# A two-layer attention and pooling trunk on one core: operand offsets in attention, a norm spread one chunk later, squares and running sums reordered, last scalings split up

## The chip, the cores and the metric

The kernel runs on 1 core of one Trainium2 chip. The metric is the device time of one execution in microseconds (us); the median of several runs counts. The engines of the core work side by side, each through its own queue in order: TensorE (PE, with its weight loads as PEld), VectorE (DVE), ScalarE (ACT), GpSimd (POOL) and SyncE (SP, which only issues transfers here). They wait for each other through semaphores.

## The reference

The input `x` is one sequence of 512 positions by 1024 channels in float32. Two layers follow each other, and each sub-layer adds its result to `x`:

```
x = x + dilated_attention_mixer(rmsnorm(x, attn_norm), w_qkv, w_attn_out)   # 24 heads in 3 groups
x = x + swiglu_ffn(rmsnorm(x, ffn_norm[0]), w_gate_up[0], w_down[0])        # d_ff = 2816
x = x + pooling_mixer(rmsnorm(x, pool_norm), w_pool_in, w_pool_group, pool_scale)
x = x + swiglu_ffn(rmsnorm(x, ffn_norm[1]), w_gate_up[1], w_down[1])
return rmsnorm(x, final_norm)
```

`rmsnorm` divides each position by the root of the mean of its squares over the channels. The pooling mixer projects to 4 groups of 256 channels, takes in each group the mean over the last 2, 4, 8 or 16 positions minus the position itself, and applies a 256 x 256 map per group. All arithmetic is float32.

## The kernel before

**Layout.** The state is held transposed: eight tiles `X[0..7]`, each 128 channels by 512 positions. A product is 128 output channels by 512 positions in one PSUM tile (`ps`, 8 buffers) and runs over the eight chunks of the contraction.

**Three matmuls for one.** A float32 operand is split into a rounded part and the rest (`split`, line 92: ACT writes the rounded part at L93, DVE subtracts it at L94). Every chunk then takes three matmuls: high weight by high operand, high by low, low by high. In `Product.add` these are L314, L315 and L317, with 512 columns each. Large products are done with fewer multiplications on quarter blocks (Strassen's scheme): `mult` issues L446, L447 and L448 with 256 columns each, and the sums of blocks are made on DVE. `values12` does the same for the values of attention (L617 to L619), with the weights as the moving operand and the activations as the stationary one.

**Weights.** They stream from memory into rings `raw` and `rawhalf` (SP's queue, and for sums of blocks POOL's) and are split into rings `w` (5 buffers) and `half`. A ring buffer is 64 float32 elements (`LINE`) longer than the weights, and `shift` says at which element of a partition's row the weights begin. `pairs(..., shift=LINE // 4)` puts the weights of attention's block products at element 16.

**Operands.** Split operands lie in slots of 2 x 512 elements in two rooms, `near` and `far`; a slot taken with `apart=True` begins `APART` = 28 elements later. The feed-forward layers use it, attention doesn't: its operands (`near`, `h`, and `tx` in the tiles of `X`) begin at element 0. So the moving operand begins 16 elements (64 bytes) below its weights in attention's block products, 28 elements (112 bytes) above them in the feed-forward layers and in `values12`, and at the same offset in plain products. All other steps of these buffers are multiples of 256 bytes.

**Order.** Instructions are written in one program; a scheduler lays them out per engine by its own priorities, so their order on an engine is not always that of the code. Stages follow each other:

1. Start (0 to 33 us): for each chunk k, `X[k]` and the weights of four products are loaded, split, and multiplied; `square(0, k)` squares the chunk on ACT (L367) and adds it up on DVE (L369).
2. Attention (to 480 us): heads two by two, with block products (`seven`), and between their steps scores, softmax and outputs of the head before, as small matmuls.
3. Feed-forward 0 (to 809 us), pooling (to 868 us), feed-forward 1 (to 1170 us). The norm between two stages is `finish`: it ends two products that were begun ahead, adds up the squares of a column over the partitions by matmuls with `ones` (`rstd`, L396), takes the power -1/2 on POOL (L402), runs three chunks of a further product (`begin(1, layer, range(3))`), and spreads the factors over the partitions by matmuls with the identity (`spread`, L409). Consumers scale the products by that `row` when they leave PSUM.
4. Pooling: `pool(g)` for g = 3, 2, 1, 0 takes two products each (L1217), makes the sum over the last 2^(g+1) positions by g + 1 shifted additions on DVE (L1225), finishes the mean (L1229 to L1233) and splits it; `mix(g)` multiplies by the group's map, adds to `X` (L1242), and makes the operands (L378 on ACT, L379 on DVE) and squares of the next norm. The order is pool 3, pool 2, mix 3, pool 1, mix 2, pool 0, mix 1, mix 0.
5. End (from 1170 us): the last five down products are done by halves of the positions (`end`, `add`: L1280 adds to `X`, L1282 squares on ACT, L1318 adds up). `emit(0, r)` scales the eight tiles of the first half (L1291) and writes them out (L1292). The second half is scaled by the norm weight (`scale_last`, L1305 or L1303), turned by PE (`turn_last`, L1313), multiplied by the factor (L1349, L1351) and written out (L1352).

The sums of the pooling windows, and the first norm's order, are these lines:

```
for k in range(KC):
    ...
    nc.scalar.activation(hi[:, s], raw[:, s], AF.Copy)
    scaled(0, k, *U[k], on_dve=k == 0)
    nc.vector.tensor_tensor(lo[:, s], raw[:, s], hi[:, s].bitcast(F32), op=OP.subtract)
    for i, f in enumerate(lead):
        f.w = (hi, lo)
        f.add([k], pos=k % 2 * NF + i - k)
    square(0, k)
```

Of the kernel before, what the change touches and what calls it, by code (L numbers as in the profile page):

```python
# [8 lines left out]
F32 = mybir.dt.float32  # L9
# [6 lines left out]
P = 128  # L16
# [31 lines left out]
LINE = 64  # L48
APART = 28
# [15 lines left out]
def trunk(ctx: ExitStack, tc: tile.TileContext, xT, xN, norms, w_first, w_qk, w_qkp, w_v0, w_v0p, w_v12, w_out, w_pair, w_down, w_dblock, w_pin, w_pgrp,  # L65
# [7 lines left out]
    def x_tile(k, name="x", dtype=F32):  # L73
        return cpool.tile([P, S], dtype, tag=f"x{k}", name=name)

    X = [x_tile(k) for k in range(KC)]
    nrm = cpool.tile([P, NORMS, KC], F32, name="nrm")
# [7 lines left out]

    tmp.tile([P, 64], F32, name="shift", bufs=1)
# [141 lines left out]
    for h in range(HEADS):  # L228
# [11 lines left out]
        else:  # L240
            pairs(w_v12[h // 2, 0], w_v12[h // 2, 1], shift=APART)
# [83 lines left out]
    def slot(name, dtype=F32R, apart=False, open=False, far=False):  # L325
# [12 lines left out]
        i = next(i for i in order if i not in taken and (i in loose or taken.get(i + 1) is not False if apart else i in loose or not taken.get(i - 1)))  # L338
        if i in loose:
            taken[i] = None  # L340
            t = cpool.tile([P, 2 * S + LINE], dtype, tag=f"slot{i}", name=name, bufs=1)
            o = APART * apart
            return i, t[:, o:o + 2 * S].rearrange("p (e c) -> p e c", e=2)
        taken[i] = apart
        o = (i - FIXED * (i >= FIXED)) * 2 * S + APART * apart
# [75 lines left out]
    def finish(lead, layer, ks):  # L421
# [4 lines left out]
        lead += begin(1, layer, range(3))  # L426
        row = row_of(spread(r))
        lead[-1].add(range(3, KC))
# [156 lines left out]
    with tc.tile_pool(name="opool", bufs=1) as opool:  # L585
        early = opool.tile([P, HEADS, S], F32R, tag="o", name="early")
        with tc.tile_pool(name="apool", bufs=1) as apool:
# [255 lines left out]
            def prepare(k):  # L843

                h, t = normed(0, k, rows["row"], Held("raw"), Held("raw"))
                for i in range(2):
                    held["h", k + i * K2], b = slot("h")
# [19 lines left out]
            def halve(h):  # L867
# [3 lines left out]
                else:  # L871
                    held["o", h], b = slot("oh", open=h == 3)
# [15 lines left out]
            for k in range(KC):  # L888
# [8 lines left out]
                nc.scalar.activation(hi[:, s], raw[:, s], AF.Copy)  # L897
                scaled(0, k, *U[k], on_dve=k == 0)
                nc.vector.tensor_tensor(lo[:, s], raw[:, s], hi[:, s].bitcast(F32), op=OP.subtract)
# [105 lines left out]
    with tc.tile_pool(name="fpool", bufs=2) as fpool:  # L1005
# [13 lines left out]
        def ffn(layer, nxt, lead, row):  # L1019
# [21 lines left out]
            def prepare(k):  # L1041
# [4 lines left out]
                held["t", k, 0], b = slot("tb", apart=True)  # L1046
                split(b[:, 0].rearrange("p (a c) -> p a c", a=2), b[:, 1].rearrange("p (a c) -> p a c", a=2), hq[:, :, 0])
                T["11", k], T["21", k] = (tuple(b[:, e, i * H2:(i + 1) * H2] for e in range(2)) for i in range(2))
                for i, names in enumerate((("1", "2"), ("3", "4"))):
                    held["t", k, 1 + i], b = slot("tt", apart=True)  # L1050
# [3 lines left out]
                if k % 2 == 0:  # L1054
                    held["t", k, 3], T["n"] = slot("tn", apart=True)
# [8 lines left out]
            def place(name, i):  # L1064
                held["d", name, i], b = slot("d" + name, apart=True)
# [143 lines left out]
        def pool(g):  # L1209
            Y[g] = []  # L1210
            for c in range(2):
# [6 lines left out]
                cur, both = u, []  # L1218
                for e in range(g + 1):
                    sh = 1 << e  # L1220
                    if e < 2:
                        both.append(ftile(f"s{e}", PAD + S))
                        nc.vector.memset(both[e][:, :PAD], 0.0)
                    s = both[e % 2]
                    nc.vector.tensor_add(s[:, PAD:], cur[:, PAD:], cur[:, PAD - sh:PAD - sh + S])  # L1225
                    cur = s
                w = WINDOWS[g]
# [57 lines left out]
        def emit(half, r):  # L1285

            cols = halves[half]
            pr = spread(r)
            for k in range(KC):
                y = X[k][:, cols]  # L1290
                nc.vector.scalar_tensor_tensor(y, y, nrm[:, 4, k:k + 1], pr[:, :H2], op0=OP.mult, op1=OP.mult)  # L1291
                nc.sync.dma_start(outT[k], y)  # L1292
# [49 lines left out]
        scale_last(KC - 1, on_dve=True)  # L1342
# [94 lines left out]
```

## Time and profile before

| | |
|---|---|
| median of 3 runs | 1197.54 us (1196.87 to 1197.91) |
| profiled execution | 1197.8 us, of which the span of the core's instructions is 1196.0 us |
| granted TensorE clock | 0.998 |
| busy in the span | PE 1184.6 us, PEld 1118.9, DVE 997.2, ACT 680.7, POOL 147.0 |
| memory | read 184.70 MB, written 2.10 MB: 156 GB/s over the span |

[...] In a row of the timeline the first number is the start, the second the duration, and a bracket tells how long the engine sat idle before and what released it. In a row of busy time by stretches, the number after x is how many instructions of the engine touch the stretch.

### The profile page before, as it was taken

The numbers are of one execution on the slowest core, as the hardware profiler recorded it, in microseconds if no ns is written. First come the engines' busy times: TensorE is split into PE (matmuls) and PEld (weight loads), VectorE is DVE, ScalarE is ACT, GpSimd is POOL, SyncE is SP. The second block draws the span as 40 slices with busy tenths as digits, with TensorE's granted clock in tenths as the row PEclk, the third lists the DMA queues.
The fourth block names the chain that finished last, engine by engine and source line by source line (L and its number), as shares of the span: only waits on it lengthen the run. The fifth ranks groups of instructions, "written<-read, shape, count | busy, mean of one in ns | idle before, by whom it ended". The sixth has DMA issues, their size and how long they took to land.

```text
span 1196.0 us, 24858 instructions
## 1 busy us (share of the span) xinstructions
PE 1184.6 (99%) x9936; PEld 1118.9 (94%) x9936; DVE 997.2 (83%) x1730; ACT 680.7 (57%) x1214; POOL 147.0 (12%) x137
## 2 busy tenths in 40 slices
PE   9999999999999999999999999999999999999997
PEld 7889999999999988898999999998789999999996
DVE  6978898889788856895899889998989998898875
ACT  6445564555456643562677567763455776676553
POOL 1111211111111000101111111100310111111100
PEclk9999999999999999999999999999999999999999
DMA  8346656665766533336677777753153777777732
GB/s 277 124 103 163 156 154 161 170 159 150 189 149 163 163 133 122 88 115 158 160 197 188 194 201 199 186 171 124 53 122 93 191 196 198 196 191 199 189 86 72
DMA packets 73365, 188.42 MB, mean 158 GB/s; under 512 B 7312, under 2 KB 9504, under 8 KB 73248
## 3 DMA queue, kind: packets, MB, share of 16 engines
q1 hardware_dynamic: 50400, 141.98, 36.1%
q0 software_dynamic: 22704, 44.58, 23.1%
q8 instruction: 78, 1.28, 0.4%
q14 instruction: 39, 0.32, 0.1%
q10 hardware_dynamic: 144, 0.26, 0.1%
HBM read 184.70 MB, written 2.10 MB: 156 GB/s over the span
## 4 chain that ended last, share of the span: by engine, by line
PE 87%; DVE 6%; issue 3%; ACT 1%; DMA 1%; POOL 0%; SPq 0%; POOLq 0%; DVEq 0%; ACTq 0%
PE ps L446 19%; PE ps L447 18%; PE ps L448 18%; PE ps L314 7%; PE ps L315 7%; PE ps L317 7%; PE ps L617 2%; PE ps L619 2%; PE ps L618 2%; DVE w L94 2%; PE ps L829 1%; PE ps L701 1%; DVE s L1225 1%; ACT w L93 1%; PE ps L721 1%
## 5 line engine op out<-in xcount | busy, mean ns | idle before, releaser
L93 ACT ACTIVATE w<-raw 128x1024 fp32r<-128x1024 f32 (+1 forms) x299 | 313.5, 1056 | 213.7 <-PE ps L448 69.1
L94 DVE TENSOR_TENSOR w<-raw,w 128x1024 fp32r<-128x1024 f32 (+1 forms) x299 | 361.5, 1214 | 58.9 <-ACT w L93 55.5
L446 PE MATMUL ps<-far,w 128*128 128x256 f32 x916 | 251.9, 275 | 0.1
L447 PE MATMUL ps<-far,w 128*128 128x256 f32 x916 | 251.8, 275 | 0.0
L448 PE MATMUL ps<-far,w 128*128 128x256 f32 x916 | 251.8, 275 | 0.0
L446 PE MATMUL ps<-near,w 128*128 128x256 f32 x632 | 178.4, 282 | 0.4 <-ACT first L528 0.4
L447 PE MATMUL ps<-near,w 128*128 128x256 f32 x632 | 174.8, 277 | 0.0
L448 PE MATMUL ps<-near,w 128*128 128x256 f32 x632 | 174.8, 277 | 0.0
L446 PEld LDWEIGHTS ps<-far,w 128*128 128x128 f32 x916 | 171.8, 188 | 0.6 <-ACT first L528 0.5
L447 PEld LDWEIGHTS ps<-far,w 128*128 128x128 f32 x916 | 171.9, 188 | 0.1
L448 PEld LDWEIGHTS ps<-far,w 128*128 128x128 f32 x916 | 171.9, 188 | 0.0
L446 PEld LDWEIGHTS ps<-near,w 128*128 128x128 f32 x632 | 118.9, 188 | 1.3 <-ACT first L528 0.9
L447 PEld LDWEIGHTS ps<-near,w 128*128 128x128 f32 x632 | 118.8, 188 | 0.0
L448 PEld LDWEIGHTS ps<-near,w 128*128 128x128 f32 x632 | 118.8, 188 | 0.0
L315 PE MATMUL ps<-near,w 128*128 128x512 f32 (+1 forms) x284 | 106.6, 375 | 0.6 <-DVE near L379 0.6
L314 PE MATMUL ps<-near,w 128*128 128x512 f32 (+1 forms) x284 | 106.9, 377 | 0.0
L317 PE MATMUL ps<-near,w 128*128 128x512 f32 (+1 forms) x284 | 106.1, 374 | 0.0
L161 POOL DMA_DIRECT2D raw<-w_pair x36 | 43.6, 1212 | 359.7 <-DMA raw<-w_pair 174.8
L315 PEld LDWEIGHTS ps<-near,w 128*128 128x128 f32 x284 | 53.4, 188 | 11.0 <-DVE near L379 1.8
L317 PEld LDWEIGHTS ps<-near,w 128*128 128x128 f32 x284 | 53.3, 188 | 9.5
L314 PEld LDWEIGHTS ps<-near,w 128*128 128x128 f32 x284 | 53.3, 188 | 9.4
L93 ACT ACTIVATE half<-rawhalf 128x512 fp32r<-128x512 f32 x81 | 51.0, 631 | 14.7 <-PE ps L448 12.5
(315 smaller groups left out, 2749.7 us busy)
## 6 DMA issues: line engine op xcount, KB each, us to landing
raw<-w_pair SPq DMA_DIRECT2D x80, 512.0 KB, 4.3
raw<-w_qkp SPq DMA_DIRECT2D x36, 512.0 KB, 4.1
raw<-w_pair POOLq DMA_DIRECT2D x36, 512.0 KB, 7.4
raw<-w_dblock SPq DMA_DIRECT2D x32, 512.0 KB, 4.5
raw<-w_v SPq DMA_DIRECT2D x18, 512.0 KB, 4.4
raw<-w_qkp POOLq DMA_DIRECT2D x18, 512.0 KB, 7.5
rawhalf<-w_pair SPq DMA_DIRECT2D x36, 256.0 KB, 5.1
raw<-w_dblock POOLq DMA_DIRECT2D x16, 512.0 KB, 7.3
```

The costliest lines, as they stand in the source:

```text
L93: nc.scalar.activation(hi, v, AF.Copy)
L94: nc.vector.tensor_tensor(lo, v, hi.bitcast(F32), op=OP.subtract)
L161: nc.gpsimd.dma_start(self.b.rearrange("p (a c) -> p a c", a=2), self.src[:, None, 3 * n:].to_broadcast([P, 2, n]), accum_op=OP.add)
L314: nc.tensor.matmul(self.p[:, cols], w[0][:, s], mh[:, cols], start=self.done == 0, stop=False)
L315: nc.tensor.matmul(self.p[:, cols], w[0][:, s], ml[:, cols], start=False, stop=False)
L317: nc.tensor.matmul(self.p[:, cols], w[1][:, s], mh[:, cols], start=False, stop=self.done == self.n)
L446: nc.tensor.matmul(dst, w.t[0][:, c], th, start=k == 0 and not on, stop=False, skip_group_check=on)
L447: nc.tensor.matmul(dst, w.t[0][:, c], tl, start=False, stop=False, skip_group_check=on)
L448: nc.tensor.matmul(dst, w.t[1][:, c], th, start=False, stop=k == n - 1, skip_group_check=on)
L617: nc.tensor.matmul(o, mh, wh, start=k == 0, stop=False)
L618: nc.tensor.matmul(o, mh, wl, start=False, stop=False)
L619: nc.tensor.matmul(o, ml, wh, start=False, stop=k == K2 - 1)
```

## The change

Five edits, which are independent in the code:

- **Attention offsets.** The weights of attention's block products begin at element 0 (`shift=0`), and their operands at element 16 (`ASIDE`): slots are taken with `apart=16`, the `X` tiles get 16 elements more in the first one so that the `tx` tiles all begin 64 bytes later, and the weights of `values12` move from 28 to 44 (`VALUES`). `slot` now keeps offsets in elements and fits neighbours by them. The moving operand begins 64 bytes above its weights in attention's block products; in `values12` and in the feed-forward layers the distance stays 112 bytes. In the plain products with `w_out`, 96 matmuls get 64 bytes as well.
- **Norm spreads.** In `finish` four chunks instead of three run between the sums of squares and the spread.
- **First squares and matmuls.** In the start, the squares of chunk k - 1 stand behind the matmuls of chunk k, and the twelve matmuls of a chunk run as four high-high, four high-low and four low-high ones.
- **Running sums.** For the windows 8 and 16 one scan, s[t] = s[t-1] + u[t] - u[t-w], replaces the three or four additions.
- **Last scalings.** `emit` returns a function, and the eight scalings of the first half with their transfers are called in groups of 3, 1, 1 and 3 between the steps of the second half.

```diff
+ASIDE = 16
+VALUES = 44
     def x_tile(k, name="x", dtype=F32):
-        return cpool.tile([P, S], dtype, tag=f"x{k}", name=name)
+        aside = ASIDE * (k == 0)
+        return cpool.tile([P, S + aside], dtype, tag=f"x{k}", name=name)[:, aside * (name == "tx"):][:, :S]
...
-    def pairs(*srcs, shift=LINE // 4, back=False):
+    def pairs(*srcs, shift=0, back=False):
...
-            pairs(w_v12[h // 2, 0], w_v12[h // 2, 1], shift=APART)
+            pairs(w_v12[h // 2, 0], w_v12[h // 2, 1], shift=VALUES)
...
+        def fits(i):
+            before, behind = taken.get(i - 1), taken.get(i + 1)
+            return i not in taken and (i in loose or (before or 0) <= apart and (behind is None or apart <= behind))
...
     def finish(lead, layer, ks):
         for f in lead:
             f.add(ks)
         r = rstd([acc[layer]])
-        lead += begin(1, layer, range(3))
+        lead += begin(1, layer, range(4))
         row = row_of(spread(r))
-        lead[-1].add(range(3, KC))
+        lead[-1].add(range(4, KC))
...
-                    held["h", k + i * K2], b = slot("h")
+                    held["h", k + i * K2], b = slot("h", apart=ASIDE)
...
-                        held["t", k, i], b = slot("t")
+                            held["t", k, i], b = slot("t", apart=ASIDE)
...
-                    held["o", h], b = slot("oh", open=h == 3)
+                    held["o", h], b = slot("oh", apart=ASIDE * (h > 3), open=h == 3)
...
-                nc.scalar.activation(hi[:, s], raw[:, s], AF.Copy)
-                scaled(0, k, *U[k], on_dve=k == 0)
+                if k:
+                    scaled(0, k, *U[k])
+                    nc.scalar.activation(hi[:, s], raw[:, s], AF.Copy)
+                else:
+                    nc.scalar.activation(hi[:, s], raw[:, s], AF.Copy)
+                    scaled(0, k, *U[k], on_dve=True)
                 nc.vector.tensor_tensor(lo[:, s], raw[:, s], hi[:, s].bitcast(F32), op=OP.subtract)
-                for i, f in enumerate(lead):
-                    f.w = (hi, lo)
-                    f.add([k], pos=k % 2 * NF + i - k)
-                square(0, k)
+                for j, (w, v) in enumerate(((hi, 0), (hi, 1), (lo, 0))):
+                    for i, f in enumerate(lead):
+                        c = (k % 2 * NF + i) * P
+                        nc.tensor.matmul(f.p, w[:, c:c + P], U[k][v], start=k == j == 0, stop=k == KC - 1 and j == 2)
+                if k:
+                    square(0, k - 1)
+            square(0, KC - 1)
...
-                cur, both = u, []
-                for e in range(g + 1):
-                    sh = 1 << e
-                    if e < 2:
-                        both.append(ftile(f"s{e}", PAD + S))
-                        nc.vector.memset(both[e][:, :PAD], 0.0)
-                    s = both[e % 2]
-                    nc.vector.tensor_add(s[:, PAD:], cur[:, PAD:], cur[:, PAD - sh:PAD - sh + S])
-                    cur = s
-                w = WINDOWS[g]
+                cur, w = u, WINDOWS[g]
+                if g < 2:
...
+                else:
+                    cur = ftile("s", PAD + S)
+                    nc.vector.tensor_tensor_scan(cur[:, PAD:], u[:, PAD:], u[:, PAD - w:PAD - w + S], 0.0,
+                                                 op0=OP.add, op1=OP.subtract)
...
-        emit(0, r)
+        out = emit(0, r)
+        out(range(3))
         for k in range(KC - ENDS + 2):
             scale_last(k)
         t = total(t, add(2, 1, end(2, 1, range(HALF // 2, HALF), f)))
+        out(range(3, 4))
...
         scale_last(KC - 1, on_dve=True)
+        out(range(4, 5))
         r = rstd([t, sq])
+        out(range(5, KC))
         turn_last(range(5, KC))
```

The scheduler's order follows at two places. First DVE's queue in the pooling stage, from the first product that leaves PSUM (`u<-ps,row`); `s` are the window sums, `far<-raw,far` splits the group maps, `w<-raw,w` splits streamed weights. Before:

```order
L1217 TENSOR_TENSOR u<-ps,row 128x512 x2
L94 TENSOR_TENSOR far<-raw,far 128x512 x2
L1225 TENSOR_TENSOR s_9917<-u 128x512
L94 TENSOR_TENSOR far<-raw,far 128x512 x2
L94 TENSOR_TENSOR w<-raw,w 128x1024
L1225 TENSOR_TENSOR s_9920<-s_9917 128x512
L1225 TENSOR_TENSOR s_9969<-u 128x512
L1225 TENSOR_TENSOR s_9917<-s_9920 128x512
L1225 TENSOR_TENSOR s_9972<-s_9969 128x512
L1225 TENSOR_TENSOR s_9920<-s_9917 128x512
L1225 TENSOR_TENSOR s_9969<-s_9972 128x512
L1229 TENSOR_TENSOR mean<-s_9920,invcnt 128x16
```

The same place of the changed kernel, on DVE (the scan is listed as SCALAR_TENSOR_TENSOR at L1249):

```order
L1239 TENSOR_TENSOR u<-ps,row 128x512
L96 TENSOR_TENSOR far<-raw,far 128x512 x2
L1249 SCALAR_TENSOR_TENSOR s<-u 128x512
L96 TENSOR_TENSOR far<-raw,far 128x512 x2
L96 TENSOR_TENSOR w<-raw,w 128x1024
L1252 TENSOR_TENSOR mean<-s,invcnt 128x16
L1254 SCALAR_TENSOR_TENSOR u<-s,u 128x496
```

Seven additions stand ahead of the first mean before, those of both halves of the group among them; now one scan stands there.

Second the end, on DVE, from the sum `total` behind the second half's second product. `x<-x,nrm,ps` are the scalings of the first half, `x<-x,ps` the additions of the second half's products, `var` begins the last norm factor. Before:

```order
L1318 TENSOR_TENSOR total<-total,sq 128x256
L1291 SCALAR_TENSOR_TENSOR x<-x,nrm,ps 128x256 x8
L1280 TENSOR_TENSOR x<-x,ps 128x256 x3
L1318 TENSOR_TENSOR total<-total,sq 128x256
L1303 TENSOR_SCALAR ends<-x,nrm 128x256
L1318 TENSOR_TENSOR total<-total,sq 128x256
L399 TENSOR_SCALAR var<-ps 128x2
L1351 TENSOR_SCALAR ends<-ps,rcol 128x512 x2
```

The same place of the changed kernel, on DVE:

```order
L1315 SCALAR_TENSOR_TENSOR x<-x,nrm,ps 128x256 x3
L1303 TENSOR_TENSOR x<-x,ps 128x256
L1315 SCALAR_TENSOR_TENSOR x<-x,nrm,ps 128x256
L1303 TENSOR_TENSOR x<-x,ps 128x256
L1344 TENSOR_TENSOR total<-total,sq 128x256
L1315 SCALAR_TENSOR_TENSOR x<-x,nrm,ps 128x256
L1344 TENSOR_TENSOR total<-total,sq 128x256
L1303 TENSOR_TENSOR x<-x,ps 128x256
L1315 SCALAR_TENSOR_TENSOR x<-x,nrm,ps 128x256
L1329 TENSOR_SCALAR ends<-x,nrm 128x256
L1315 SCALAR_TENSOR_TENSOR x<-x,nrm,ps 128x256
L405 TENSOR_SCALAR var<-ps 128x2
```

The three additions no longer stand behind eight scalings; seven scalings stand ahead of `var`, and the eighth behind it, ahead of the last two `ends<-ps,rcol`.

On PE the last sums of squares (`ones`) also stand earlier among the turns (`ident,ends`). Before:

```order
L317 MATMUL ps<-near,w 128x256
L1313 MATMUL ps<-ident,ends 128x128 x14
L396 MATMUL ps<-ones,total 32x1 x8
L396 MATMUL ps<-ones,sq 32x1 x8
L1313 MATMUL ps<-ident,ends 128x128 x2
```

The same place of the changed kernel, on PE:

```order
L319 MATMUL ps<-near,w 128x256
L1339 MATMUL ps<-ident,ends 128x128 x10
L402 MATMUL ps<-ones,total 32x1 x8
L402 MATMUL ps<-ones,sq 32x1 x8
L1339 MATMUL ps<-ident,ends 128x128 x6
```

Ten turns instead of fourteen stand ahead of the sums.

More of the change, by code (lines that the diff above doesn't have):

```diff
@@ L323, in trunk, with slot @@
     room, taken = {}, {}
-    def slot(name, dtype=F32R, apart=False, open=False, far=False):
+    def slot(name, dtype=F32R, apart=0, open=False, far=False):
         top, low = range(FIXED + SLOTS - 1, FIXED - 1, -1), range(FIXED, FIXED + SLOTS)
@@ L337, in slot @@
             order = [*low, *near, *loose] if far else [*near, *low, *loose]
-        i = next(i for i in order if i not in taken and (i in loose or taken.get(i + 1) is not False if apart else i in loose or not taken.get(i - 1)))
+        def fits(i):
+            before, behind = taken.get(i - 1), taken.get(i + 1)
+            return i not in taken and (i in loose or (before or 0) <= apart and (behind is None or apart <= behind))
+        i = next(i for i in order if fits(i))
         if i in loose:
@@ L1285, in emit, with out @@
         def emit(half, r):
-            cols = halves[half]
             pr = spread(r)
[L1289 to L1292, printed above, removed]
+            def out(ks):
+                for k in ks:
+                    y = X[k][:, halves[half]]
+                    nc.vector.scalar_tensor_tensor(y, y, nrm[:, 4, k:k + 1], pr[:, :H2], op0=OP.mult, op1=OP.mult)
+                    nc.sync.dma_start(outT[k], y)
+            return out
         scaled_last, turned = {}, {}
```

29 lines of the change are left out of this document (21 added, 8 removed).

## The prediction

> **What bounds the kernel now.** I read the page's busy times, clock and chain first.
>
> ```profile
> PE 1184.6 (99%) x9936; PEld 1118.9 (94%) x9936; DVE 997.2 (83%) x1730; ACT 680.7 (57%) x1214; POOL 147.0 (12%) x137
> PEclk9999999999999999999999999999999999999999
> PE 87%; DVE 6%; issue 3%; ACT 1%; DMA 1%; POOL 0%; SPq 0%; POOLq 0%; DVEq 0%; ACTq 0%
> ```
>
> PE is busy at full clock nearly throughout, and the chain that ended last is 87% PE. So time can be won only where its matmuls follow each other slower than elsewhere, or where PE waits. For the first I read PE's busy time by stretches.
>
> ```profile
> 120.60:126.90 6.30, 6.30 (x58) 1.00 0.66 127
> 153.10:164.30 11.20, 11.20 (x97) 1.00 0.67 162
> 255.60:266.80 11.20, 11.20 (x98) 1.00 0.66 166
> 357.95:369.15 11.20, 11.20 (x97) 1.00 0.63 159
> 600.00:611.20 11.20, 11.20 (x101) 1.00 0.73 178
> 874.00:910.00 36.00, 36.00 (x161) 1.00 0.40 90
> ```
>
> A listed matmul of 256 columns lasts 0.28 us, so two or three more touch a stretch than start in it. In feed-forward 0 (600 to 611 us) 99 start in 11.2 us: one per 113 ns. In attention (153, 255 and 358 us, the same place of three pairs of heads) only 95 start: 118 ns. At 120 us attention has 113 ns too. A slow stretch begins and ends with an interruption, a small matmul of softmax or scores. Short ones lie between; this is the first and the last start of 24 in a row, 2.71 us for 23 steps, 118 ns again:
>
> ```profile
> 112.00 0.28 PE L446 MATMUL ps<-near,w 128*128 128x256 f32 x1
> ...
> 114.71 0.28 PE L448 MATMUL ps<-h,w 128*128 128x256 f32 x1
> ```
>
> For the second I read the timeline at the start, the norms, the pooling stage and the end; these rows stand at the parts.
>
> **Attention offsets.** The three long stretches hold 3 x 95 matmuls, at 4.7 ns too much 1.3 us; the short ones I estimate at 0.7 to 1.1 us from the one quoted, as it and like ones return with each pair of heads. So about 2.2 us can go. Which distance between moving operand and weights is good, the trace shows at three: at -64 bytes (attention before) a stretch can stay slow; at +112 bytes (feed-forward) it doesn't; at 0 bytes (plain products, 512 columns, 874 to 910 us) 159 start in 36 us, 226 ns, twice 113. The new +64 lies between 0 and 112, both good, so I take it as good. What is left is the run-in after an interruption, seen at +112 in feed-forward 1:
>
> ```profile
> 939.07 0.28 PE L447 MATMUL ps<-far,w 128*128 128x256 f32 x1
> ...
> 939.90 0.28 PE L448 MATMUL ps<-far,w 128*128 128x256 f32 x1
> ```
>
> Seven steps take 0.83 us there, 5 ns each too much, before 113 ns is back: 0.03 us per interruption. Attention's block products have, as an estimate, some 40 of them, a dozen for each of the pairs of heads, since small matmuls stand between most of their steps; many already pay more than that. I subtract half of 40 x 0.035 and take a gain of 1.5 us; the bounds are 2.5 us and, below nothing, the slower rival. The longer tiles and the 96 plain products with 64 bytes cost nothing that a row shows: no transfer or instruction is added.
>
> [...]
>
> **The start.** PE waits in the third chunk, 11.46 to 13.21 us, where plain pitch is 0.227 us:
>
> ```profile
> 11.46 0.39 PE L317 MATMUL ps<-early,w 128*128 128x512 f32 x1
> 11.91 0.50 PE L314 MATMUL ps<-early,w 128*128 128x512 f32 x1
> 12.25 0.40 PE L315 MATMUL ps<-early,w 128*128 128x512 f32 x1
> 12.86 0.51 PE L317 MATMUL ps<-early,w 128*128 128x512 f32 x1 [0.22 <-DVE w L899]
> 13.21 0.39 PE L314 MATMUL ps<-early,w 128*128 128x512 f32 x1
> 11.25 0.61 ACT L897 ACTIVATE w<-raw 128x512 fp32r<-128x512 f32 x1
> 12.12 0.69 DVE L899 TENSOR_TENSOR w<-raw,w 128x512 fp32r<-128x512 f32 x1
> ```
>
> The first two excesses (0.22 and 0.11 us) wait for ACT's high part, ready at 11.86. The scheduler gives ACT the same order as before, squares ahead of weights in the first chunks, although the code now puts the squares later; so these stay. The last two (0.38 and 0.12) wait for DVE's low part, ready at 12.81. With the low-high matmuls last, it is wanted eight matmuls after 11.91, at 13.7. Gain 0.5 us, between 0 and 0.85. The squares' sums end long before the `ones` matmuls want them.
>
> **The norm spreads.** PE waits for POOL's power ahead of each spread:
>
> ```profile
> 485.16 0.71 PE L409 MATMUL ps<-ident,rcol 128*128 128x128 f32 x4 [0.39 <-POOL rcol L402]
> 811.76 0.39 PE L317 MATMUL ps<-far,w 128*128 128x512 f32 x1
> 812.54 1.37 PE L409 MATMUL ps<-ident,rcol 128*128 128x128 f32 x8 [0.40 <-POOL rcol L402]
> 872.04 1.37 PE L409 MATMUL ps<-ident,rcol 128*128 128x128 f32 x8 [0.16 <-POOL rcol L402]
> 486.50:523.00 36.50, 36.46 (x61) 1.00 0.26 64
> ```
>
> A chunk more is three matmuls, 0.68 us, enough to cover all of them (at 812 us the start comes 0.55 us later than 0.227 after the one before, 0.40 of it listed as idle). But the row itself comes when POOL is done, as before, and who waits for it is DVE. At 485 us DVE is then busy without a gap to 523 us (last row), and PE's first block product follows it closely; PE would come half a microsecond early and wait there. I count nothing for this spread, with bounds of a 0.55 us gain and a 0.1 us loss, as the spread's first half starts later. At 812 us the half microsecond counts if the pooling stage does not give it back (next part). At 872 us before's scheduler already had four chunks there; the changed order puts `var` ahead of one of two weight splits that DVE did first, which ends the wait: 0.16 us, and with the restart in the proportion of 812 us some 0.3.
>
> **Running sums.** In the pooling stage DVE is the late one:
>
> ```profile
> 814.60:865.50 50.90, 49.98 (x101) 1.00 0.28 90
> 850.00:868.50 18.50, 17.83 (x73) 1.00 0.10 30
> L1225 DVE TENSOR_TENSOR s<-s 128x512 f32<-128x512 f32 x12 | 8.0, 683 | 0.0
> 819.93 0.68 DVE L1225 TENSOR_TENSOR s<-s 128x512 f32<-128x512 f32 x1
> 820.53 0.69 DVE L1225 TENSOR_TENSOR s<-u 128x512 f32<-128x512 f32 x1
> 854.05 0.50 PE L315 MATMUL ps<-near,w 128*128 128x512 f32 x1 [0.31 <-DVE near L379]
> ```
>
> DVE is busy 49.98 of 50.9 us. PE starts some 71 matmuls in 850 to 868.5 us, where 81.5 fit at 0.227: 2.4 us lost, all behind DVE's results but for 0.2 us around the `ones`. The change takes out 14 additions (2 halves x 4 and 2 x 3) at a pitch of 0.60 us (819.93 to 820.53), 8.4 us, and puts in 4 scans. No row has a scan; it can't be under one addition, 0.60 us, and would at 2.1 us eat all it saves. I take two additions, 1.2 us, since it does two operations per element, the second feeding the first. That leaves 8.4 - 4.8 = 3.6 us less on DVE, more than PE's 2.4 us plus the 0.56 from the spread. Followed through the new order, DVE catches up with PE at the last pooling product, and only what follows `mix(0)` stays a chain. I take 1.75 of the 2.4 us, and with the spread's 0.55 a gain of 2.3 us; bounds 3.0, and 0 if the scan is dear.
>
> [...]
>
> **The end.** These rows carry it:
>
> ```profile
> 1182.24 3.21 DVE L1291 SCALAR_TENSOR_TENSOR x<-x,nrm,ps 128x256 f32<-128x256 f32 x8
> 1185.38 1.08 DVE L1280 TENSOR_TENSOR x<-x,ps 128x256 f32<-128x256 f32 x3
> 1187.25 0.40 ACT L1282 ACTIVATE sq<-x 128x256 f32<-128x256 f32 x1
> 1188.35 0.16 DVE L399 TENSOR_SCALAR var<-ps 128x2 f32<-128x2 f32 x1 [0.94 <-PE ps L396]
> 1188.59 1.05 POOL L402 TENSOR_TENSOR rcol<-var,nhalf 128x1 f32<-128x1 f32 x2 [7.84 <-DVE var L399]
> 1189.16 1.41 DVE L1351 TENSOR_SCALAR ends<-ps,rcol 128x512 f32<-128x512 f32 x2 [0.65 <-POOL rcol L402]
> 1185.40 1.73 PE L1313 MATMUL ps<-ident,ends 128*128 128x128 f32 x12
> 1182.74 3.78 SPq L1292 DMA_DIRECT2D out<-x  x8
> 1189.88 1.30 SPq L1352 DMA_DIRECT2D out<-ends  x3
> ```
>
> Eight scalings (0.40 us each) hold up three additions whose products PE has ended by 1185.4. The last addition starts near 1186.0, its square on ACT ends at 1187.65, and `var` follows 0.7 us later. Now the last addition can start at 1185.5, when its product is done, and ACT has no heap of squares: the square ends near 1186.4, and the sums stand behind 10 turns, not 14. DVE has two scalings and one `ends` in between, ready by 1187.1. So `var` comes at about 1187.1, 1.25 us earlier. The eighth scaling behind `var` (0.4 us) fits under POOL's first half, 0.8 us from `var` to L1351. Against it, transfers of the first half are issued later on SP (0.47 us each, 3.78 by 8), the last near 1188.0, still ahead of the first output of the second half, one of 1.3 us by 3. I take 1.0 us, with bounds of a 1.3 us gain and a 0.3 us loss, if those transfers crowd the last ones.
>
> **The sum.** 1.5 + 0.5 + 0.0 + 2.3 + 0.3 + 1.0 = 5.6 us. The profiled execution took 1197.8 us, of which its span is 1196.0; less 5.6 it is 1192.2. The median of the runs, 1197.54, lies 0.26 lower, so I predict 1191.9 us.
>
> **The rivals.**
>
> [...]
> - *The scan is dear, or DVE is not what PE waits for.* From 2.1 us a scan upwards DVE is as late as before, and the 0.55 us of the spread is waited away. For it: no row has a scan. Against the second half: the row at 854 us that names DVE, and DVE's full stretch. 3.3 us is won: 1194.2.
> - *Slower: +64 bytes is a bad distance.* The 21 block products of attention have 84 matmuls each (seven steps, four chunks, three matmuls), 1764. If all ran at 118 ns, that is 8.3 us instead of 2.2, and the rest of the change, 4.1 us, is not enough: 1199.5, within 0.2%. If the loss is twice that, 9.4 ns, it is 16.6 us and the time 1207.8. It decides from 4.9 ns per matmul, (4.1 + 2.2 + 2.4) / 1764. Against it: 0 and 112 bytes are both good; for it, those are other shapes and tiles, and no row has +64.
> - *Parts of the code change don't reach the engines.* ACT's order at the start already shows one; if the end gave nothing as well, it would be 1192.9, inside the first range.
>
> **How the numbers follow.** 0.2%, 2.4 us, is about what a measurement of this kernel can tell from no change. The forecast has a chance of 0.62 with a range of its own of 1189.2 to 1194.2 (gains of 8.3 to 3.3 us, the bounds without their last extremes). Offsets without effect have 0.14, a dear scan 0.10, and +64 bytes bad 0.14, of which 0.06 ends within 0.2% and 0.08 slower. Of the forecast's chance 0.02 falls within 0.2% as several parts may fail together, and another 0.02 goes slower through a new wait in the feed-forward layers, whose DVE queue is nearly full. So faster 0.82, same 0.08, slower 0.10. The range goes from 1189.2 to 1196.0: both faster rivals are in it, up to one with both effects gone (1195.7), and the bad distance is left out.
>
> **What would show it.** Right: in the changed profile, stretches of attention with 99 starts in 11.2 us throughout; no excess behind L918 near 12.9 us; spreads that wait for nothing; a scan near 1.2 us, and PE starts at 0.227 us from 850 us on; `var` about 1.2 us closer to PE's last product. Wrong: 118 ns over whole heads; scans above 2 us; PE rows in the pooling stage that still name DVE; last transfers that land later after L1381 than now after L1351. A new wait of over 0.5 us where the first block product of a feed-forward layer meets DVE would show that the gain of a spread was only moved.

## The result: slower by 0.1%, and the profile after

The changed kernel takes 1198.39 us (median, 1197.77 to 1200.78), the kernel before in the same session 1197.4 (1196.77 to 1198.09): a ratio of 1.001, with a 95% interval of 1.0002 to 1.0018. Forecast were 1191.9 us. In the profiled executions the spans are 1196.0 us before and 1196.3 after; this pair differs by 0.3 us, the medians by 1.0.

The page after shows the same bound at the same clock; PE's busy time has grown by 1.3 us:

```profile
PE 1185.9 (99%) x9936; PEld 1123.0 (94%) x9936; DVE 995.9 (83%) x1712; ACT 681.3 (57%) x1214; POOL 147.3 (12%) x137
PEclk9999999999999999999999999999999999999999
PE 91%; DVE 5%; issue 2%; ACT 1%; DMA 0%; POOL 0%; DVEq 0%; POOLq 0%; SPq 0%; ACTq 0%
```

The matmuls with `ones` end each stage, so their starts in the timeline of PE divide the span. Before:

```profile
28.96 0.43 PE L396 MATMUL ps<-ones,sq 128*32 128x1 f32 x32
481.57 0.43 PE L396 MATMUL ps<-ones,sq 128*32 128x1 f32 x32
809.44 0.43 PE L396 MATMUL ps<-ones,sq 128*32 128x1 f32 x32
868.50 0.43 PE L396 MATMUL ps<-ones,sq 128*32 128x1 f32 x32
1178.89 0.31 PE L396 MATMUL ps<-ones,total 128*32 128x1 f32 x16
```

After:

```profile
28.07 0.43 PE L402 MATMUL ps<-ones,sq 128*32 128x1 f32 x32
484.74 0.43 PE L402 MATMUL ps<-ones,sq 128*32 128x1 f32 x32
812.03 0.43 PE L402 MATMUL ps<-ones,sq 128*32 128x1 f32 x32
870.11 0.43 PE L402 MATMUL ps<-ones,sq 128*32 128x1 f32 x32
1180.01 0.31 PE L402 MATMUL ps<-ones,total 128*32 128x1 f32 x16
```

Differences of neighbouring rows give the stages, in us:

| stage, with the part of the change in it | before | after | change | forecast |
|---|---|---|---|---|
| start, to the first norm (squares, matmul order) | 28.96 | 28.07 | -0.89 | -0.5 |
| attention and output projection (offsets) | 452.61 | 456.67 | **+4.06** | **-1.5** |
| layer-1 norm, feed-forward 0 (spread) | 327.87 | 327.29 | -0.58 | 0.0 |
| layer-2 norm, pooling (spread, running sums) | 59.06 | 58.08 | -0.98 | -2.3 |
| layer-3 norm, feed-forward 1 (spread) | 310.39 | 309.90 | -0.49 | -0.3 |
| end, to the end of the span (scalings) | 17.11 | 16.29 | -0.82 | -1.0 |
| sum | 1196.0 | 1196.3 | +0.3 | -5.6 |

Without attention the parts won 3.76 us in this pair of profiles, where 4.1 were forecast (in the medians of the runs below it is 3.0); attention alone turned the sign. One stretch shows how. Busy time by stretches at 182 to 193.2 us, where a run of block products of attention stands in both kernels, before and after (behind the length stand PE, PEld, DVE, ACT and POOL, then the granted clock, the share of the DMA engines and GB/s):

```profile
182.00:193.20 11.20, 11.20 (x102) 11.20 (x100) 9.63 (x16) 6.38 (x14) 1.29 (x1) 1.00 0.43 82
```
```profile
182.00:193.20 11.20, 11.20 (x97) 11.20 (x96) 9.96 (x16) 5.84 (x13) 1.29 (x1) 1.00 0.39 80
```

PE touches 102 matmuls before and 97 after (a listed one of 256 columns lasts 0.28 us, so several overlap): 113 ns from start to start have become 118. A step is the distance of two neighbouring starts, both of 256 columns; it counts as slow when the next start comes 2.2 to 9 ns later than 113.4. Of the 1728 steps of attention's block products 29% were slow before, with 2.21 us lost, and 74% are now, with 5.66 us. The slow steps aren't strewn about. Of the 36 stretches with twelve or more steps between two interruptions (other products or small matmuls), 9 are slow throughout and 27 fast before, 29 slow and 7 fast after, each from its ninth step on, and none is mixed. So at both offsets a stretch can take either pitch and then keeps it; the new offset makes the slow one the usual one. The products with `w_out`, of which half got 64 bytes, lose another 0.6 us: of their 191 steps 131 last 229 ns or more, where 227 is usual; before it was 19.

The scan's row, one line of the trace:

```profile
L1249 DVE TENSOR_TENSOR_SCAN s<-u x4: 1216/1218/1218, 819.0 to 831.3; 128x512 f32<-128x512 f32 x4
```

It takes 1.218 us, the 1.2 us of the forecast and about two additions at the pitch of 0.60 us seen before. By listed durations it is 1.8 additions of 0.683 us (L1225 before).

### The profile page after: what moved, and what is told of

The parts are those of the page before. It is cut to its first block, busy times and chain, and to the rows that moved or that the text cites. A ratio compares the mean times of both kernels' runs of the same rounds, so it can differ in the third digit from the quotient of the medians.

```text
span 1196.3 us, 24834 instructions
## 1 busy us (share of the span) xinstructions
PE 1185.9 (99%) x9936; PEld 1123.0 (94%) x9936; DVE 995.9 (83%) x1712; ACT 681.3 (57%) x1214; POOL 147.3 (12%) x137
## 4 chain that ended last, share of the span: by engine, by line
PE 91%; DVE 5%; issue 2%; ACT 1%; DMA 0%; POOL 0%; DVEq 0%; POOLq 0%; SPq 0%; ACTq 0%
PE ps L452 19%; PE ps L453 18%; PE ps L454 18%; PE ps L316 7%; PE ps L317 7%; PE ps L319 7%; PE ps L623 2%; PE ps L625 2%; PE ps L624 2%; PE ps L922 2%; DVE w L96 2%; PE ps L835 1%; PE ps L707 1%; DVE far L96 1%; PE ps L829 1%
```

## The experiments

All stand against the kernel before; a kernel derived from the changed one is to be compared with its 1198.39 us. "Attention" is the time from the first to the second row of `ones`.

### Which edit lost the 4 us

**off_back**: the changed kernel with the old offsets.

```diff
-ASIDE = 16
-VALUES = 44
+ASIDE = 0
+VALUES = 28
...
-    def pairs(*srcs, shift=0, back=False):
+    def pairs(*srcs, shift=16, back=False):
```

> The changed kernel with the attention offsets of before (operands at 0, weights 64 bytes on, distance -64 bytes); all other edits stay. Attention with the output projection, from the first matmul of the first norm's sum to that of the second norm, took 452.6 us before and 456.7 us after. Theory 1, the distance of +64 bytes sets the slow pitch: it is 452.6 again, the stretches of block products at 118 ns are as rare as before, and the time is about 1194.4 us. Rival, the loss comes through the other edits (the earlier start shifts the gaps in attention, and the slow pitch falls elsewhere by chance): it stays near 456.7 and the time near 1198.4.

Measured: 1194.54 us, ratio 0.9975 (0.9965 to 0.9985).

**before_off**: the kernel before with the offset edit alone, as in the diff of the change.

> The kernel before with the attention offsets alone (+64 bytes). Theory 1: attention with the output projection takes 456.6 us, three quarters of the block products' matmuls start 118 ns apart, the 512-column products of the output projection partly 231 ns, and the time is about 1201.4 us. Rival: 452.6 us and 1197.4.

Measured: 1201.19 us, ratio 1.0031 (1.0019 to 1.0043). The first two `ones` rows of both, off_back first:

```profile
28.75 0.43 PE L402 MATMUL ps<-ones,sq 128*32 128x1 f32 x32
481.34 0.43 PE L402 MATMUL ps<-ones,sq 128*32 128x1 f32 x32
```
```profile
28.43 0.43 PE L402 MATMUL ps<-ones,sq 128*32 128x1 f32 x32
485.09 0.43 PE L402 MATMUL ps<-ones,sq 128*32 128x1 f32 x32
```

Attention takes 452.59 us with the old offsets among the new edits, and 456.66 with the new offsets among the old ones. The other edits shift nothing there: that the offset edit costs the 4 us holds to 0.1 us in both directions, and the rival falls. Whether it is the distance, as theory 1 says, or the places, these two runs can't tell, since the edit moves both. The shares of slow steps repeat as well, 29% and 74%. off_back is also a measurement of the other four edits together: 3.0 us won against the kernel before of the same session (1197.54), of 4.1 forecast; and before_off has the offsets alone, 3.65 us lost.

### What makes an offset bad

Nine further placements, by edits of the three numbers above and, where it is said, of the `x` tiles or of `oh`.

**off_112**: weights moved, `shift=52`.

> The changed kernel with the weights of the block products moved on by 208 bytes, so that operands stand +112 bytes from them, counted modulo 256, as in feed-forward; one number is changed. Theory 1, with the distance counted modulo 256: block products start 113 ns apart but for the run-in of some six steps behind an interruption; of the 5.7 us by which 1764 matmuls were too slow at most 1.5 us stays, attention with the output projection takes about 452 us or less, and the time is 1194 or less. The other answer, that the loss is not from the distance, or that it isn't counted modulo 256: near 456.7 and 1198.4.

**off_0**: `ASIDE = 0`, `shift=0`, `VALUES = 28`.

> The changed kernel with operands and weights of the block products both at offset 0, distance 0 bytes. The prediction took 0 as a good distance from plain products of 512 columns. If that carries over to 256 columns: as at +112, a time of about 1193 to 1194. If a distance near 0 is bad there: 118 ns over most block products and 1198 or more.

**off_240**: `ASIDE = 28`, `shift=0`, `VALUES = 56`, all `x` tiles 32 elements longer.

> The changed kernel with attention's moving operands at 112 bytes and its weights at 0, the very places of feed-forward; the x tiles are made 128 bytes longer for it, so that half of the tx tiles stand at 240 bytes as feed-forward's do, the other half at 112. Before: 84 to 98% of attention's matmuls slow with the same distance of 112 made by moving the weights. Theory 2, the place of each operand counts (the moving one off the 64-byte grid, the weights on it): nearly none is slow but for the run-in; attention with the output projection 449 to 451 us, time 1191 to 1193. Rival, what is slow is the work of attention itself (short stretches between interruptions), whatever the places: over half of the matmuls slow, time 1197 or more.

**off_48**: `ASIDE = 12`, `shift=0`, `VALUES = 40`, all `x` tiles 16 elements longer.

> As the run with 112 bytes, but with 48: moving operands of the near and h tiles at 176 bytes (modulo 256), tx tiles at 48, 112, 176 and 240, weights at 128. Theory 2, moving operands off the 64-byte grid: as good as 112, time 1191 to 1193. Rival, only the pair of feed-forward (240 and 128) is good: near and h matmuls slow in half or more of the steps, time 1196 or more.

**off_192_other**: `ASIDE = 48`, `shift=0`, `VALUES = 12`.

> The changed kernel with moving operands at 192 bytes past and weights at 0: the distance of before, -64 bytes modulo 256, made in another way (64 and 128 modulo 256 where before had 128 and 192). If the distance modulo 256 decides: a quarter to a third of the matmuls slow, time 1194.5 as with the old offsets. If it is the single places: another share, and a time away from 1194.5 by over 1 us.

**off_96**: `ASIDE = 24`, `shift=0`, `VALUES = 52`.

> The changed kernel with moving operands at 96 bytes, weights at 0 (224 and 128 modulo 256; on the 32-byte grid, off the 64-byte grid). Theory 2 with a grid of 64 bytes: good, 1191 to 1193. With a grid of 32 bytes: slow as at +64 (three quarters and more of the matmuls), 1198 or more.

**off_160**: `ASIDE = 40`, `shift=0`, `VALUES = 4`, and `slot("oh", apart=ASIDE * (h in (4, 5)), ...)`.

> The changed kernel with attention's moving operands at 160 bytes from the weights (32 and 128 modulo 256), and the halved heads of the output projection at 0 where the slots allow it (heads 3, 6 and 7; 4 and 5 at 160). Theory 3, with weights on a 32-byte grid and 256 columns the distance modulo 256 decides, and the good ones lie between 112 and 192 bytes (seen so far: 0, 48, 64 and 96 bad, 112 and 192 good, 240 bad): under 12% of the block products slow, and with fewer odd distances in the output projection than in the run at 192 a time of 1192 to 1193. Rival, no such rule, 192 and 112 are single good points: over half slow, 1198 or more.

**off_192_third**: weights moved, `shift=32`.

> The changed kernel with only the weights of the block products moved, by 128 bytes: operands at 192, weights at 0 modulo 256, distance -64 for the third time, in a third place. If -64 is what is good for these products: attention with the output projection 451.5 to 453 us, time 1193 to 1194.6. If the place decides: 456 us or more, 1198 or more.

**off_224**: `ASIDE = 56`, `shift=0`, `VALUES = 20`.

> The changed kernel with attention's operands at 224 bytes from the weights (96 and 128 modulo 256), the neighbour of -64 on the other side than 160. If -64 stands alone: over half of the steps slow, attention with the output projection over 456 us, 1198 or more. If the good stretch reaches from 192 upwards: as at -64, 1193.

What they measured. Places are bytes modulo 256 in a partition; slow is the share of attention's block-product steps as counted above, and lost the time of these.

| kernel | operand, weights | distance | slow | lost, us | attention, us | median, us (interval of the ratio) |
|---|---|---|---|---|---|---|
| off_192_other | 64, 128 | -64 | 8% | 0.6 | 451.8 | 1193.10 (0.9953 to 0.9978) |
| off_back (as before) | 128, 192 | -64 | 29% | 2.2 | 452.6 | 1194.54 (0.9965 to 0.9985) |
| off_192_third | 192, 0 | -64 | 41% | 3.1 | 454.2 | 1196.31 (0.9979 to 0.9997) |
| the changed kernel | 192, 128 | +64 | 74% | 5.7 | 456.7 | 1198.39 (1.0002 to 1.0018) |
| off_240 | 240, 128; half of `tx` 112, 128 | +112; -16 | 50% | 4.4 | 458.7 | 1200.37 (1.0014 to 1.0036) |
| off_160 | 32, 128 | -96 | 87% | 7.5 | 458.9 | 1200.75 (1.0017 to 1.0039) |
| off_224 | 96, 128 | -32 | 88% | 7.3 | 459.6 | 1200.99 (1.0018 to 1.0043) |
| off_112 | 192, 80 | +112 | 86% | 8.5 | 460.0 | 1201.37 (1.0021 to 1.0049) |
| off_0 | 128, 128 | 0 | 97% | 10.7 | 461.3 | 1203.26 (1.0033 to 1.0063) |
| off_96 | 224, 128 | +96 | 63% | 5.3 | 462.4 | 1203.44 (1.0040 to 1.0070) |
| off_48 | 176, 128; `tx` mixed | +48 and others | 94% | 8.2 | 463.3 | 1204.92 (1.0050 to 1.0080) |

Where a time exceeds the lost column, other products of attention suffer too: in off_96 larger gaps of over 9 ns, in off_240 and off_48 the products of `values12`, of whose steps 96 and 93% are slow (8 to 12% in the other kernels).

Theory 1's extension (the distance modulo 256 decides, and 0 and 112 are good) fell with off_112 and off_0. Theory 2 (operand off the 64-byte grid) fell with off_48 and off_96, theory 3 (all from 112 to 192 is good) with off_160. What stands: of all kernels tried, the three with -64 bytes in attention have the fewest slow steps, and the neighbours 32 bytes to either side are bad. But the three aren't equal (8, 29, 41%). off_192_other's 1193.10 us lies over 1 us from 1194.5, which had been named as the sign that the places count, and off_192_third fell between its two answers. So the distance isn't all that decides; the places count as well. The same at +112: it is good in feed-forward, with the weights at 128, and bad in off_112, with the weights at 80. off_240 meant to put attention at feed-forward's places, but half of its `tx` tiles got -16, and half of all steps are slow. Its trace still tells something of a clean +112: the steps on `near` and `h`, which stand at feed-forward's places, are nearly all slow at first behind a `tx` operand or an interruption, and from the twelfth step on only 3 of 396 are. So +112 does settle at 113 ns in attention too, after a run-in; what a kernel with every operand there would take wasn't measured. Why a placement is good is open.

**ffn_64**: the same distance in feed-forward, one number.

```diff
-APART = 28
+APART = 16
```

> The changed kernel with feed-forward's moving operands at +64 bytes instead of +112; attention as in the changed kernel. If +64 is bad for such block products wherever they stand, some 4370 matmuls of feed-forward 0 and 1 start about 118 ns apart in three quarters of the steps or more: 15 to 20 us more, 1213 to 1219. If it is bad only between attention's interruptions: not over 2 us more, 1198.4 to 1200.

Measured: 1216.71 us, ratio 1.0157 (1.0144 to 1.0171). The stretch of 600 to 611.2 us, after (the changed kernel) and with +64:

```profile
600.00:611.20 11.20, 11.20 (x101) 11.20 (x100) 10.07 (x17) 8.00 (x14) 1.21 (x1) 1.00 0.76 200
```
```profile
600.00:611.20 11.20, 11.20 (x97) 11.20 (x97) 9.74 (x18) 7.72 (x13) 1.88 (x2) 1.00 0.68 168
```

99 starts become 95, and of 4365 steps in the two feed-forward layers, up to the last stage, 99.9% are slow instead of 2%: 19.1 us lost in these steps, 18.3 us more in the median. So +64 is bad in feed-forward as well as in attention, and where attention's interruptions are missing nearly every step is slow: one run of slow steps is 2184 long.

### The pooling stage

The chain behind PE's waits after, from the timeline, PE first:

```profile
854.47 0.39 PE L316 MATMUL ps<-near,w 128*128 128x512 f32 x1
855.50 0.50 PE L317 MATMUL ps<-near,w 128*128 128x512 f32 x1 [0.64 <-DVE near L385]
856.07 0.40 PE L316 MATMUL ps<-near,w 128*128 128x512 f32 x1
857.20 0.50 PE L317 MATMUL ps<-near,w 128*128 128x512 f32 x1 [0.73 <-DVE near L385]
854.70 2.45 DVE L385 SCALAR_TENSOR_TENSOR near<-x,nrm,near 128x512 fp32r<-128x512 f32 x2
857.07 1.24 DVE L1252 TENSOR_TENSOR mean<-s,invcnt 128x2 f32<-128x2 f32 x1
854.94 3.35 POOL L375 TENSOR_TENSOR sq<-sq 128x512 f32<-128x512 f32 x2 [10.28 <-issue]
```

PE's starts at 855.50 and 857.20 come 0.80 and 0.90 us later than 0.227 after the one before. They wait for L385, a low part on DVE, and there single DVE operations take far longer than elsewhere: two of the low parts take 2.45 us while POOL adds squares, and a `mean` of 128 x 2 elements takes 1.24 us. All eight of each line:

```profile
L385 DVE SCALAR_TENSOR_TENSOR near<-x,nrm,near x8: 743/750/1696, 841.5 to 866.3; 128x512 fp32r<-128x512 f32 x8
L1252 DVE TENSOR_TENSOR mean<-s,invcnt x8: 150/162/1242, 822.4 to 857.1; 128x16 f32<-128x16 f32 x2, 128x8 f32<-128x8 f32 x2, 128x4 f32<-128x4 f32 x2, 128x2 f32<-128x2 f32 x2
```

The numbers are the shortest, the median and the longest in ns: 0.74 us and, at worst, 1.70 for the low part, 0.15 and 1.24 for the mean. The long ones of both lines stand beside POOL's additions (L375, 854.94 to 858.29 and 861.07 to 864.42). That POOL holds them is the author's theory from these rows; the next runs test it.

**pool_adds**: the running sums undone, as in the diff of the change read backwards.

> The changed kernel with the running sums undone (additions for all four widths, as before). The prediction's term: the scans were worth 1.75 us, so 1200.1 us. Rival from the trace of the changed kernel: they were worth 0.1 us, because what is late in the last pooling products is a chain behind POOL's sums of squares, so 1198.5, and the two stalls of 0.8 and 0.9 us stand or become many small ones of the same sum.

Measured: 1199.04 us, ratio 1.0015 (1.0005 to 1.0024); 58.86 us from norm to norm (811.72 to 870.58) against 58.08. So the scans were worth 0.78 us in this stage, between the two numbers expected (1.75 and 0.1), and the spread 0.20, what is left of the 0.98 if nothing else of the change acts there.

**pool_sum_dve**: the sums of squares on DVE.

```diff
-                square(3, m, nc.gpsimd)
+                square(3, m)
```

> The changed kernel with the sums of squares of layer 3's chunks added on DVE instead of POOL: 7 additions of about 0.6 us more on DVE, none on POOL. Theory: the low parts (0.74 us alone, 1.70 us where POOL's addition runs beside them) are held by POOL; without it they take 0.74 us throughout, the stalls of 0.8 and 0.9 us at 854 and 856 us fall to under 0.4 us together or each, and 1 us or so is won: 1197.4. Rival, DVE's amount of work counts: 4.2 us more of it is late by as much as before or more, 1198.4 to 1200.

Measured: 1196.93 us, ratio 0.9995 (0.9986 to 1.0004), and 56.79 us from norm to norm (811.97 to 868.76). The answer for L385, and PE's start that waited 0.64 us:

```profile
L385 DVE SCALAR_TENSOR_TENSOR near<-x,nrm,near x8: 742/744/752, 841.4 to 865.4; 128x512 fp32r<-128x512 f32 x8
855.02 0.50 PE L317 MATMUL ps<-near,w 128*128 128x512 f32 x1 [0.22 <-DVE near L385]
```

No low part takes over 0.75 us, the second stall is gone, and 1.29 us is won although DVE has seven additions more. The row at 855.02 comes 0.38 us late where the two before came 1.70 us late in all, so the gain lies at these two starts. The theory holds.

### The end

**end_old**: all eight scalings in one place again (`out(range(KC))` behind `emit`, the four calls taken out).

> The changed kernel with the eight last scalings in one place again. By the traces of before and after, splitting them brought var 1.2 us closer to the last product, and the last transfers took 0.35 us longer from the last scaling to the end of the span. Theory: both go back, span 0.8 us longer, 1199.2. Rival, the split gave nothing: 1198.4, with var as close as now.

Measured: 1198.84 us, ratio 1.0013 (1.0003 to 1.0022), alone too near to the changed kernel to count; the traces tell it. The last `var`, the last scaling and the outputs, after:

```profile
1188.30 0.16 DVE L405 TENSOR_SCALAR var<-ps 128x2 f32<-128x2 f32 x1
1189.11 1.41 DVE L1381 TENSOR_SCALAR ends<-ps,rcol 128x512 f32<-128x512 f32 x2 [0.27 <-POOL rcol L408]
1189.82 1.39 SPq L1382 DMA_DIRECT2D out<-ends  x3
```

And in end_old, with the first half's `ones`:

```profile
1179.86 0.31 PE L402 MATMUL ps<-ones,total 128*32 128x1 f32 x16
1189.31 0.16 DVE L405 TENSOR_SCALAR var<-ps 128x2 f32<-128x2 f32 x1 [0.94 <-PE ps L402]
1190.12 1.41 DVE L1378 TENSOR_SCALAR ends<-ps,rcol 128x512 f32<-128x512 f32 x2 [0.66 <-POOL rcol L408]
```

From the first half's `ones` to `var` it is 8.29 us after (1180.01 to 1188.30) and 9.45 in end_old: the split wins 1.16 us. Between the two halves' `ones` the same is 7.70 us in all fifteen profiles with the split and 8.87 or 8.88 in the three without. From the last scaling to the span's end it is 7.19 us after, 6.68 in end_old (span 1196.8) and 6.84 before, so this pair gives back 0.35 to 0.5. That part scatters: from the last `ones` to the span's end the split kernels take 7.74 to 9.45 us (median 8.41), the others 8.07 to 8.23. A loss of some 0.2 us at the transfers is likely but not shown, nor is that they crowd each other.

### A better kernel

**best_combo**: the changed kernel with off_192_other's numbers, `oh` as in off_160, and the sums on DVE.

> The changed kernel with three edits: attention's operands at 192 bytes from weights at 0 (distance -64 bytes modulo 256, 1193.1 us by itself), the halved heads of the output projection at 0 but for heads 4 and 5, and the sums of squares of layer 3's chunks on DVE (1.3 us less from norm to norm in the pooling stage). Expected: the first as before, the second takes 0.4 to 0.7 us out of the output projection, where products with 512 columns were 233 ns apart in half the steps, the third 1.3 us: 1191.2. If the gains don't add, 1192 to 1193.

Measured: 1191.48 us, ratio 0.9949 (0.9935 to 0.9962), 0.3 us from the 1191.2 expected and faster than both kernels. The stretch at 182 us:

```profile
182.00:193.20 11.20, 11.20 (x101) 11.20 (x100) 10.33 (x15) 7.21 (x15) 1.29 (x1) 1.00 0.53 128
```

8% of the block-product steps are slow, attention takes 451.47 us (28.12 to 479.59), so the `oh` places brought 0.3 us and not 0.4 to 0.7, and pooling 56.79.

## Why the prediction was wrong, point by point

- **Attention offsets, the step that failed.** "The new +64 lies between 0 and 112, both good, so I take it as good." The step from two good distances to one between them failed, and one of the two wasn't good for these products. The 0 was read from 512-column products at 226 ns; with 256 columns it has the most slow steps of all in attention, 97%, at 120 ns. The 112 is good only at some places. And nothing good was found between: 48, 64 and 96 are all bad. The size of what could be won was right (2.2 us estimated, 2.21 counted before), and off_192_other shows that 1.6 of it can be had, by the old distance in another place. The rival "+64 bytes is a bad distance" described what happened: it gave 6.1 us of loss with all steps slow and 1199.5 us; three quarters of the steps are, and it is 3.45 us in block products, 4.06 with the output projection. The 96 plain products with 64 bytes, put at no cost, are in the difference of 0.6. The rival had 0.14; "those are other shapes and tiles" spoke for it, and was the sentence to weigh more. That offsets have no effect was given 0.14 too; the offset edit alone cost 3.65 us (before_off).
- **Spreads.** Mechanism right: in none of the three does PE wait any more. Sizes: layer 1 was put at 0.0 because DVE is full behind it. DVE is full (36.46 of 36.50 us behind it before, 36.50 after), and its first use of the row comes no earlier (4.97 us behind `ones` before, 4.96 after), yet PE keeps the 0.58 us, so the forecast's "PE would come half a microsecond early and wait there" is wrong: PE was not tied to DVE there. Layer 3 gave 0.49 for 0.3, layer 2 0.20 for 0.55. Layers 1 and 3 repeat: with feed-forward's offsets as they were, the two stages take 327.3 to 327.5 and 309.9 us in every profile with the spread edit, 327.9 and 310.4 in both without it.
- **Running sums.** The scan's length was right, and DVE's work fell. The 1.75 us assumed that PE waits for the amount of work on DVE, since DVE was busy 49.98 of 50.9 us. Part of that busy time was spent in operations that last longer beside POOL's additions: before, a low part took up to 1.69 us there (L379, median 0.75). 0.78 us came, and moving POOL's sums brought 1.29 more.
- **Start.** -0.89 in this pair, but not shown. The time from the first plain product to the first `ones` scatters from 21.98 to 22.79 us over the sixteen profiles of the new start, and the two of the old one have 22.97 and 22.26. In the changed kernel's profile ACT still does squares ahead of weights in the third chunk, as forecast, but the waits behind ACT are gone there together with those behind low parts, where the forecast said that they stay: from 10.30 us on, fifteen matmuls start 226 or 227 ns apart. A gain of more than a few tenths isn't established.
- **End.** `var` comes 1.16 us earlier, where 1.25 were forecast, and this repeats to 0.01 us. The stage won 0.82 for 1.0; what the last transfers gave back, named as a bound of 0.3 us, lies within their scatter.
- **The range** reached to 1196.0 and left the bad distance out, the only case that happened. No row had a 256-column product at +64, so nothing bounded the offset term from below; both ends, 2.5 us won and 6 lost, belonged into the range.

## What to carry to other kernels

Read the distance of matmul starts, not busy time: 113, 118 and 120 ns all show as a PE that is busy for 200.00 of 200.00 us at a granted clock of 1.00 (200 to 400 us before, after and in off_0). An address offset that is good for one shape need not be good for another: here 0 is good with 512 columns (226 ns) and the worst with 256 (120 ns), and in off_192_other, where -64 is best with 256 columns, the 96 matmuls of 512 columns in `w_out` that also stand at -64 start 233 ns apart instead of 227. Nor are offsets to be interpolated; try the candidate in one run of its own, since it costs one number. A DVE that looks full may be held up inside its instructions, as in L385, where one form took from 0.74 to 1.70 us: compare the same operation's shortest and longest row, and look at what POOL does beside the long ones.

## What was not expected of the hardware

In these runs the place of moving operand and weights in a partition's row changed the pitch of 256-column matmuls between 113.4 and 120 ns, 6%: 97% of attention's steps are slow at distance 0 (off_0), 8% at the best place of -64 bytes (off_192_other), 99.9% of feed-forward's at +64 (ffn_64) and 2% at +112 (the changed kernel). In attention a stretch settled on one pitch in its first eight steps at +64 and at -64 and kept it until something interrupted it (36 stretches of 36 before and after); in feed-forward at +64 the slow pitch lasted 2184 steps in a row. And in the changed kernel a DVE operation of 128 x 2 elements took 1.24 us beside POOL's addition, where the shortest of its line took 0.15.
